# The first head's levels and states ahead of the split of the combined x, in one line that orders a half's mix

## The chip, the cores and the metric

The kernel runs on one core of a Trainium2 chip. Its time is the device time of one execution in microseconds (us), as a median of several runs; lower is better. Beside the runs there is one profiled execution, from which the views of the trace come. The engines are PE (matrix products, with PEld loading weights beside it), DVE (vector work), ACT (activations, copies, casts), POOL and SP (which issues most DMAs). Each has its own queue of instructions and takes them strictly in order; an instruction that waits holds up all behind it on its engine.

## The reference

One decoder layer over x of (1, 2048, 1024) in float32. Two groups of heads read the same normed x, their outputs are joined, projected and added; a gated MLP with a causal convolution follows.

```python
u = rmsnorm(h, norm_mix_w)
proj = u @ w_in                        # hq, hf, hi, hg: 4 heads of 128 each; att: 8 query heads, 2 key/value heads of 64
f = lb + (1 - lb) * sigmoid(hf)        # forget gates; k = 1 - f
o_hg = hgrn2_chunkwise(q, k, v=hi, log(f))   # S_t = diag(f_t) S_{t-1} + k_t v_t^T, o_t = S_t^T q_t
o_hg = rmsnorm(o_hg, hg_norm_w) * silu(hg)
o_att = sliding_window_attention_with_sinks(aq, ak, av, sinks)   # window of 128, blocks of 128 queries
h = h + concat(o_hg, o_att) @ w_out
v = rmsnorm(h, norm_ffn_w)
h = h + (silu(conv(v @ w_gate)) * (v @ w_up)) @ w_down
out = rmsnorm(h, final_norm_w)
```

## The kernel before

The layer runs over two halves of 1024 tokens. Each half has a mix stage (both groups of heads) and an ffn stage (out-projection `pop`, gate and up, down). The features lie on the partitions, the tokens along the free axis, so x is eight tiles of 128 by 1024. Every float32 product is made of three matmuls over rounded parts: high times high, low times high, high times low (lines 933, 934 and 935, with `whi`, `wlo` for a weight and `XH`, `XL` for x). Line 983 rounds on ACT, line 984 takes the rest on DVE.

The mix stage is written as Python generators that a loop advances by the words of the string `ORDER`:

- `H0` to `H3` are the four recurrent heads (`hgrn`), of seven steps each. Step 1 makes q and the forget gates, step 2 the products QK and the first scores in a strip, steps 3, 4 and 5 each two levels of a doubling scheme (1 to 4, 8 and 16, 32 and 64). At a level ACT copies half of QK into a tile `G` (line 718, a ring of three), DVE multiplies (line 722), and PE forms the scores of two levels in one bank, `plev` (line 704). The levels go by the length of a piece, so that of 64 is the last. Step 6 makes the values v, transposes the keys (`pkn`, line 769, copied by ACT to `Kn`) and forms the states (`pu`, line 778; DVE adds them up in `SS`, line 782). Step 7 makes the output (`po`, lines 793 and 794; normed to `on`, line 802; transposed as `pot`, line 807).
- `A0` to `A3` are pairs of attention heads (`attend`), of five steps: the projections (step 1, which also makes the gates of the recurrent heads, tile `hg`), the scores `psc` and softmax `sc` of each 512 queries (steps 2 and 3; lines 545 to 585), then for each 512 the transposes `ppt` (line 594), two masks on DVE (`pp` and `po`, line 597) and the output `poT` (line 607; steps 4 and 5).
- `W0` and `V0` prepare and form the values of the recurrent heads.
- `T0` (`Twofold.begin`) and `U0` (`Twofold.end`) serve a saving of matmuls for pairs of weights: `two_units` uses seven products of quarter size where eight would be needed (accumulators X, Y, Z and V). It needs sums and differences of pieces of x, the combined x. `T0` makes most of them in their own tiles, and `t1` aside; `U0` splits `t1` into its parts and writes them over x's own second half in `X[0]` and `X[1]`, which only the products ahead of it may still read as x.
- `S` loads and splits the finished head outputs for the out-projection.

The kernel doesn't fix each engine's order by hand. A scheduler with a timing model of its own takes the instructions in the order in which the Python code wrote them as priorities and sets each engine's queue, once, at build time. A change of `ORDER` changes these priorities, the choice of buffers and with both the queues. Banks are scarce: four PSUM banks for projections, two for the recurrent heads (`plev`, `pkn`, `pu`, `po`, `pot` share them), two for attention (`psc`, `ppt`, `poT` share them).

Of the kernel before, what the change touches and what calls it, by code (L numbers as in the profile page):

```python
# [20 lines left out]
S = 2048  # L21
# [23 lines left out]
TAIL_WARM = 7  # L45
LV = 4
ORDER = """
H0 W0 T0 H0 V0 U0 H0 A0 H0 H0 H1 A0 A0 H0 H0 H1 A0 H1 A1 H1 A0 H1 H2 A1 A1 H1 H1 H2 A1 H2 A2 H2 A1 H2 H3 A2 A2 H2 H2 H3 A2 H3 A3 H3 A2 H3 A3 A3 S H3 A3 H3 A3
"""
SPLIT = (0, 4, 1, 5, 2, 6)  # L50
DEEP = 2
# [1526 lines left out]
```

## Time and profile before

| | |
|---|---|
| Time before, median of 3 runs | 2173.33 us (2171.72 to 2174.48) |
| Profiled execution, its own time | 2180.96 us |
| Its span, first to last instruction | 2179.2 us |
| Mean granted clock of PE | 0.985 |
| PE busy | 2120.0 us, 97% of the span |
| DVE busy | 1664.7 us, 76% |
| ACT busy | 1136.6 us, 52% |
| First mix, about | 55 to 390 us of the span |
| Second mix, about | 1130 to 1475 us of the span |

A row of the timeline has the start in us from the span's first instruction, the duration in us, the engine, the line of the kernel, the operation, what it writes and reads, its size and how many like it stand together. In brackets stands the engine's idle time just ahead of it and what ended it: `[2.45 <-ACT hg L948]` says that PE stood still for 2.45 us until ACT's line 948 had written `hg`. In a row of the windows each engine has its busy time and in brackets its count of instructions; the granted clock is 1.00 at full speed.

### The profile page before, as it was taken

The numbers are of one execution on the slowest core, as the hardware profiler recorded it, in microseconds if no ns is written. First come the engines' busy times: TensorE is split into PE (matmuls) and PEld (weight loads), VectorE is DVE, ScalarE is ACT, GpSimd is POOL, SyncE is SP. The second block draws the span as 40 slices with busy tenths as digits, with TensorE's granted clock in tenths as the row PEclk, the third lists the DMA queues.
The fourth block names the chain that finished last, engine by engine and source line by source line (L and its number), as shares of the span: only waits on it lengthen the run. The fifth ranks groups of instructions, "written<-read, shape, count | busy, mean of one in ns | idle before, by whom it ended". The sixth has DMA issues, their size and how long they took to land.

```text
span 2179.2 us, 30013 instructions
## 1 busy us (share of the span) xinstructions
PE 2120.0 (97%) x11396; PEld 1747.9 (80%) x11396; DVE 1664.7 (76%) x2453; ACT 1136.6 (52%) x2007; POOL 23.8 (1%) x52
## 2 busy tenths in 40 slices
PE   9999988999999999999999999889999999999998
PEld 7887777788888888888877878668888888888887
DVE  7668887699787878785872568776998888787866
ACT  6576666464444445345744666654644344453454
POOL 1000000000000000000000000000000000000000
PEclk9999998999999999999999999889999999999999
DMA  5544332513233234964652333224132323259743
GB/s 195 185 169 173 116 108 87 188 64 126 92 105 103 100 118 159 389 214 164 224 203 100 114 110 137 86 89 144 59 135 82 126 92 113 95 189 379 247 145 131
DMA packets 116925, 319.19 MB, mean 146 GB/s; under 512 B 19626, under 2 KB 22058, under 8 KB 116780
## 3 DMA queue, kind: packets, MB, share of 16 engines
q1 hardware_dynamic: 111524, 315.42, 41.5%
q10 hardware_dynamic: 5256, 1.85, 0.3%
q8 instruction: 89, 1.46, 0.3%
q14 instruction: 56, 0.46, 0.1%
HBM read 224.21 MB, written 92.02 MB: 145 GB/s over the span
## 4 chain that ended last, share of the span: by engine, by line
PE 72%; DMA 5%; DVE 4%; ACT 4%; issue 1%; SPq 0%; ACTq 0%; DVEq 0%
PE X L1158 7%; PE X L1159 7%; PE X L1160 7%; PE pop L249 5%; PE Y L1160 4%; PE Y L1159 4%; PE Y L1158 4%; PE pdx L1376 3%; PE pdx L1377 3%; PE pdx L1378 3%; PE pdy L1377 3%; PE pdy L1376 3%; PE pdy L1378 3%; PE Z L1160 2%; PE Z L1159 2%; PE Z L1158 2%
## 5 line engine op out<-in xcount | busy, mean ns | idle before, releaser
L983 ACT CAST whi<-raw 128x1024 fp32r<-128x1024 f32 (+2 forms) x123 | 114.5, 941 | 130.4 <-PE X L1159 74.4
L984 DVE TENSOR_TENSOR wlo<-raw,whi 128x1024 fp32r<-128x1024 f32 (+2 forms) x123 | 132.3, 1080 | 9.1 <-ACT whi L983 9.1
L1158 PE MATMUL X<-T,whi 128*128 128x512 f32 x352 | 137.4, 390 | 0.0
L1159 PE MATMUL X<-T,whi 128*128 128x512 f32 x352 | 137.1, 389 | 0.0
L1160 PE MATMUL X<-T,wlo 128*128 128x512 f32 x352 | 137.0, 389 | 0.0
L1257 DVE SCALAR_TENSOR_TENSOR y<-ga,cw,y 128x1024 f32<-128x1024 f32 x88 | 112.3, 1278 | 25.7 <-ACT y L1255 25.7
L1165 ACT COPY u<-X 128x512 f32<-128x512 f32 x88 | 51.6, 587 | 120.5 <-PE X L1160 120.4
L249 PE MATMUL pop<-XH,whi 128*128 128x512 f32 x256 | 86.9, 406 | 4.5 <-ACT XH L618 1.7
L249 PE MATMUL pop<-XL,whi 128*128 128x512 f32 x256 | 87.5, 405 | 1.5 <-DVE XL L261 0.9
L984 DVE TENSOR_TENSOR xld<-raw,xhd 128x1024 fp32r<-128x1024 f32 x72 | 80.2, 1129 | 9.7 <-ACT xhd L983 9.5
L249 PE MATMUL pop<-XH,wlo 128*128 128x512 f32 x256 | 85.9, 400 | 0.0
L983 ACT CAST xhd<-raw 128x1024 fp32r<-128x1024 f32 x72 | 69.2, 979 | 29.4 <-DMA raw<-act0B 7.7
L722 DVE TENSOR_TENSOR QK<-QK,f 128x1024 f32<-128x1024 f32 x56 | 68.3, 1220 | 18.6 <-ACT G L718 18.5
L1158 PEld LDWEIGHTS X<-T,whi 128*128 128x128 f32 x352 | 66.0, 188 | 15.2 <-ACT u L1165 1.6
L1160 PEld LDWEIGHTS X<-T,wlo 128*128 128x128 f32 x352 | 66.1, 188 | 13.8
L1159 PEld LDWEIGHTS X<-T,whi 128*128 128x128 f32 x352 | 66.1, 188 | 13.7
L718 ACT COPY G<-QK 128x1024 f32<-128x1024 f32 x48 | 51.6, 1075 | 46.6 <-DVE QK L722 38.6
L1377 PE MATMUL pdx<-xld,hid 128*128 128x512 f32 x192 | 74.7, 389 | 0.0
L1376 PE MATMUL pdx<-xhd,hid 128*128 128x512 f32 x192 | 74.2, 390 | 0.0
L1378 PE MATMUL pdx<-xhd,lod 128*128 128x512 f32 x192 | 72.4, 389 | 0.0
L1160 PE MATMUL Y<-B,S 128*128 128x512 f32 x176 | 68.6, 390 | 0.0
L1160 PE MATMUL Z<-B,wlo 128*128 128x512 f32 x176 | 68.5, 389 | 0.0
(468 smaller groups left out, 6442.1 us busy)
## 6 DMA issues: line engine op xcount, KB each, us to landing
wr<-in_w_down SPq DMA_DIRECT2D x90, 512.0 KB
raw<-in_w_gate SPq DMA_DIRECT2D x44, 512.0 KB
raw<-in_w_up SPq DMA_DIRECT2D x44, 512.0 KB
raw<-act0T SPq DMA_DIRECT2D x20, 512.0 KB
raw<-act1T SPq DMA_DIRECT2D x20, 512.0 KB
act0B<-y SPq DMA_DIRECT2D x33, 256.0 KB
act1B<-y SPq DMA_DIRECT2D x33, 256.0 KB
raw<-in_w_out SPq DMA_DIRECT2D x16, 512.0 KB
```

The lines of the kernel that those rows point to most:

```text
L249: marks["unit"] = nc.tensor.matmul(o[b], w, x[:, bs], start=f, stop=l)
L718: nc.scalar.copy(G.rearrange("p t (b c m) -> p t b c m", c=2, m=m), far)
L722: done = nc.vector.tensor_tensor(own, own, Fv.rearrange("p b w -> p w b").unsqueeze(3).to_broadcast([P, 2, nb, m]), op=ALU.mult)
L983: return (nc.scalar.copy(h, src), (eng or nc.vector).tensor_tensor(l, src, h.bitcast(F32), op=ALU.subtract))
L984: (eng or nc.vector).tensor_tensor(l, src, h.bitcast(F32), op=ALU.subtract))
L1158: nc.tensor.matmul(o, wh[:, ws], xh, start=i == 0 and not more, stop=False, skip_group_check=more)
L1159: nc.tensor.matmul(o, wh[:, ws], xl, start=False, stop=False, skip_group_check=more)
L1160: r = nc.tensor.matmul(o, wl[:, ws], xh, start=False, stop=i == 3, skip_group_check=more)
L1257: nc.vector.scalar_tensor_tensor(y, g[:, w:w + HALF], C.cw[:, ft, w:w + 1], y, op0=ALU.mult, op1=ALU.add)
L1376: nc.tensor.matmul(o, wh[:, i, c], ah[:, i, cols], start=f, stop=False, skip_group_check=more)
L1377: nc.tensor.matmul(o, wh[:, i, c], al[:, i, cols], start=False, stop=False, skip_group_check=more)
L1378: nc.tensor.matmul(o, wl[:, i, c], ah[:, i, cols], start=False, stop=l, skip_group_check=more)
```

## The change

Only the string `ORDER` differs:

```diff
 ORDER = """
-H0 W0 T0 H0 V0 U0 H0 A0 H0 H0 H1 A0 A0 H0 H0 H1 A0 H1 A1 H1 A0 H1 H2 A1 A1 H1 H1 H2 A1 H2 A2 H2 A1 H2 H3 A2 A2 H2 H2 H3 A2 H3 A3 H3 A2 H3 A3 A3 S H3 A3 H3 A3
+H0 W0 T0 H0 V0 H0 H0 H0 U0 H0 A0 H1 A0 A0 H0 H1 H1 A1 H1 A0 H1 H2 A0 A1 A1 H1 H1 H2 A1 H2 A2 H2 A1 H2 H3 A2 A2 H2 H2 H3 A2 H3 A3 H3 A2 H3 A3 A3 S H3 A3 H3 A3
 """
```

The first head's steps 3, 4 and 5 (levels) and 6 (states) now stand ahead of the first attention pair, and three of them ahead of `U0`; before, `U0` stood ahead of step 3, and steps 4 to 6 stood among the first pair's. Behind that, the first pair's outputs (its steps 4 and 5) stand later: step 4 behind the second head's step 4 (before ahead of its step 3), step 5 behind the third head's first. From `A1 A1 H1 H1` on the words are the same. The same string serves both halves. The instructions that are issued are the same but for six more ACT table loads. On each engine the queues are the same up to the split in the first mix, and again in both ffn stages.

On DVE, at the split in the first mix, `t` is `t1` of the combined x. These rows stand in both kernels, at the same place of the queue; the last is the product of level 16:

```order
L984 TENSOR_TENSOR XL<-t_602,XH 128x512
L984 TENSOR_TENSOR wlo<-raw,whi 128x512 x2
L984 TENSOR_TENSOR XL<-t_617,XH 128x512
L984 TENSOR_TENSOR wlo<-raw,whi 128x512 x2
L722 TENSOR_TENSOR QK<-QK,f 128x2x32x16
```

The split did not move. The product of level 64 on DVE (`QK<-QK,f 128x2x8x64`) stood here before:

```order
L984 TENSOR_TENSOR wlo<-raw,whi 128x768
L547 TENSOR_TENSOR ql<-att_948,qh 64x512
L899 TENSOR_TENSOR raw<-raw 128x256
L903 TENSOR_TENSOR raw<-raw 128x256
L547 TENSOR_TENSOR ql<-att_948,qh 64x512
L693 COPY_PREDICATED strip<-lmask_327,odd 126x32x2
L900 TENSOR_TENSOR raw<-raw 128x256
L693 COPY_PREDICATED strip<-lmask_333,odd 124x16x4
L952 TENSOR_TENSOR att_948<-att_948,Y 128x512
L904 TENSOR_TENSOR raw<-raw 128x256
L528 SCALAR_TENSOR_TENSOR att_948<-att_948,invb 128x512
L722 TENSOR_TENSOR QK<-QK,f 128x2x8x64
```

and stands here now:

```order
L746 TENSOR_TENSOR F<-f 128x8
L528 SCALAR_TENSOR_TENSOR att_1078<-att_1078,invb 128x512
L563 MEMSET sc 128x128 x2
L722 TENSOR_TENSOR QK<-QK,f 128x2x8x64
L547 TENSOR_TENSOR ql<-att_1078,qh 64x512 x2
L693 COPY_PREDICATED strip<-lmask_327,odd 126x32x2
L984 TENSOR_TENSOR wlo<-raw,whi 128x768
L693 COPY_PREDICATED strip<-lmask_333,odd 124x16x4
L899 TENSOR_TENSOR raw<-raw 128x256
```

It came forward over the split of a weight, the low parts of the queries (`ql`) and the four sums of a combined weight (lines 899 to 904).

On PE, in the second mix, the scores of a pair in the half's early part (`psc`), and what stands ahead of them, before:

```order
L933 MATMUL X<-XH,whi 128x512
L934 MATMUL X<-XL,whi 128x512
L704 MATMUL plev<-G 64x64 x8
L704 MATMUL plev<-G 32x32 x16
L558 MATMUL psc<-KS,qh 128x256
L558 MATMUL psc<-KS,ql 128x256
```

The first scores of the same pair now:

```order
L933 MATMUL Z<-XH,whi 128x512
L558 MATMUL psc<-KS,qh 128x256
L934 MATMUL Z<-XL,whi 128x512
L935 MATMUL Z<-XH,wlo 128x512
L933 MATMUL Y<-XH,whi 128x512
L934 MATMUL Y<-XL,whi 128x512
L558 MATMUL psc<-KS,qh 128x256
L935 MATMUL Y<-XH,wlo 128x512
```

Before, a batch of eight scores stands ahead of these X products, and the next batch of eight follows right behind `plev`. Now `plev` has gone ahead, and the first scores of the batch stand singly among Z and Y products.

On PE, in the second mix's last part, the transposes `ppt` of a pair's first 512 queries and the output `poT` from them, before (`pop` is the out-projection, its numbers are accumulators):

```order
L594 MATMUL ppt<-ident,sc 128x128 x5
L249 MATMUL pop_12741<-XL,whi 128x512
L249 MATMUL pop_12742<-XL,whi 128x512
L249 MATMUL pop_12741<-XH,wlo 128x512
L249 MATMUL pop_12742<-XH,wlo 128x512
L249 MATMUL pop_12783<-XL,whi 128x512
L249 MATMUL pop_12784<-XL,whi 128x512
L249 MATMUL pop_12783<-XH,wlo 128x512
L249 MATMUL pop_12784<-XH,wlo 128x512
L704 MATMUL plev<-G 64x64 x8
L704 MATMUL plev<-G 32x32 x16
L607 MATMUL poT<-pp,V 64x128 x2
```

and now:

```order
L793 MATMUL po<-v_12534,ST 128x128
L794 MATMUL po<-SS,QK 128x128
L249 MATMUL pop_12784<-XH,wlo 128x512
L594 MATMUL ppt<-ident,sc 128x128 x8
L607 MATMUL poT<-pp,V 64x128 x2
```

Eight out-projection products and a `plev` stood between the transposes and the output. Now the output follows the transposes directly, and the out-projection products and `plev` stand ahead of both.

## The prediction

> **What bounds the kernel now.** I read the busy table first, then the clock row and the chain of waits, to see which engine sets the end.
>
> ```profile
> PE 2120.0 (97%) x11396; PEld 1747.9 (80%) x11396; DVE 1664.7 (76%) x2453; ACT 1136.6 (52%) x2007; POOL 23.8 (1%) x52
> PEclk9999998999999999999999999889999999999999
> PE 72%; DMA 5%; DVE 4%; ACT 4%; issue 1%; SPq 0%; ACTq 0%; DVEq 0%
> ```
>
> PE is busy for 2120.0 us of a span of 2179.2 us. The change adds no matmul, so it can gain only from the 59.2 us in which PE stands still, and from stretches in which the clock is low. The next view, the table of windows, shows where these lie. Its columns are the stretch and its length, busy time of PE, PEld, DVE, ACT and POOL, the granted clock, the DMA share and GB/s.
>
> ```profile
> 180.00:240.00 60.00, 55.79 (x513) 45.81 (x511) 47.86 (x101) 43.45 (x113) 1.55 (x3) 1.00 0.39 139
> 240.00:300.00 60.00, 56.71 (x469) 46.56 (x470) 47.49 (x99) 41.64 (x84) 0.00 (x0) 0.97 0.44 160
> 300.00:345.00 45.00, 34.10 (x265) 28.65 (x264) 36.17 (x72) 26.87 (x67) 1.55 (x3) 0.77 0.30 96
> 1140.00:1180.00 40.00, 39.97 (x248) 32.24 (x246) 10.78 (x15) 13.52 (x37) 0.00 (x0) 1.00 0.20 63
> 1290.00:1345.00 55.00, 51.07 (x359) 43.94 (x356) 37.15 (x80) 35.79 (x98) 2.09 (x3) 0.97 0.28 97
> 1345.00:1400.00 55.00, 51.08 (x461) 42.20 (x462) 40.61 (x84) 34.01 (x95) 1.95 (x3) 0.94 0.23 81
> 1400.00:1475.00 75.00, 60.03 (x512) 47.69 (x507) 55.62 (x112) 44.68 (x110) 0.00 (x0) 0.84 0.38 122
> ```
>
> PE's idle time in the three stretches of the first mix is 4.2, 3.3 and 10.9 us (length less busy time), and in the last three of the second 3.9, 3.9 and 15.0 us: 41.2 us of the 59.2. That is the stock from which this change draws. In both tails the clock is low as well, 0.77 and 0.84. At 1140 to 1180 us, where the second mix splits the combined x, PE stands still for 0.03 us.
>
> **The split itself: nothing.** The words of the change speak of the first head's levels standing ahead of the split. DVE's timeline at both splits, with the idle time before an instruction and its releaser in brackets:
>
> ```profile
> 96.42 0.69 DVE L984 TENSOR_TENSOR XL<-t,XH 128x512 fp32r<-128x512 f32 x1 [7.63 <-ACT XH L983]
> 102.28 1.22 DVE L722 TENSOR_TENSOR QK<-QK,f 128x1024 f32<-128x1024 f32 x1 [2.16 <-ACT G L718]
> 1175.56 1.29 DVE L984 TENSOR_TENSOR XL<-t,XH 128x512 fp32r<-128x512 f32 x2 [24.45 <-ACT XH L983]
> 1181.42 1.22 DVE L722 TENSOR_TENSOR QK<-QK,f 128x1024 f32<-128x1024 f32 x1 [4.57 <-ACT G L718]
> ```
>
> DVE had been idle for 7.63 and 24.45 us when the split came, and it idles again before the next level: the level waits for its G, not for the split. In the order of the changed kernel the split's rows stand where they stood, ahead of the product of level 16; only the product of level 64 comes forward, over some ten rows of work on weights and attention. With PE full at that place, I cost all of this at 0. If that cover were gone, the price would be the split's two pieces, 2 x 0.69 = 1.4 us in each mix. What the change does lies behind it: the first head's later products come forward in the queues, and attention goes back. The sum is over PE's waits there, one by one.
>
> **First mix.** PE's timeline at its waits, with one row of low clock (243.37) and one transpose (306.52):
>
> ```profile
> 221.38 0.38 PE L558 MATMUL psc<-KS,qh 128*128 128x256 f32 x1 [1.29 <-DVE sc L567]
> 236.87 0.44 PE L607 MATMUL poT<-pp,V 128*64 128x128 f32 x4 [0.83 <-DVE pp L597]
> 241.07 0.50 PE L933 MATMUL Y<-XH,whi 128*128 128x512 f32 x1 [2.45 <-ACT hg L948]
> 241.41 0.39 PE L934 MATMUL Y<-XL,whi 128*128 128x512 f32 x1
> 241.64 0.40 PE L935 MATMUL Y<-XH,wlo 128*128 128x512 f32 x1
> 243.37 0.63 PE L935 MATMUL Y<-XH,wlo 128*128 128x512 f32 x1
> 299.42 1.16 PE L778 MATMUL pu<-v,Kn 128*128 128x128 f32 x8 [2.21 <-ACT Kn L770]
> 306.52 0.60 PE L594 MATMUL ppt<-ident,sc 128*128 128x128 f32 x4
> 311.26 0.69 PE L607 MATMUL poT<-pp,V 128*64 128x128 f32 x4 [4.14 <-DVE pp L597]
> 327.26 0.44 PE L607 MATMUL poT<-pp,V 128*64 128x128 f32 x4 [4.00 <-DVE pp L597]
> ```
>
> (a) 221 to 241 us, together 4.6 us. In the new order the second attention output of pair 0 has whole groups of Y, X and V products between its transposes and itself, so its 0.83 us goes. The Y product that waited 2.45 us for ACT's copy has some seven products of 512 columns more ahead of it, and these follow each other in 0.23 us (241.41 to 241.64): 1.6 us. I take -0.8 - 1.6 = -2.4 us; ends -4.6 and 0.
>
> (b) 299 to 327 us, together 10.35 us. Here both orders have nearly met again. The state product pu keeps some 0.6 us more ahead of it (2.21 to 1.6). The 4.14 us wait is handed on rather than removed: with poT out of the way the next Y product stands ahead of its ACT copy, which queues behind work that came forward, some 3.0 us. The last poT keeps its round trip from ppt over two DVE masks, and one more ACT operation in it (4.00 to 4.6). -1.1 us; ends -4 and +2.
>
> **Second mix.** The same view:
>
> ```profile
> 1293.88 0.57 PE L558 MATMUL psc<-KS,qh 128*128 128x256 f32 x1 [2.80 <-DVE sc L567]
> 1307.63 1.16 PE L778 MATMUL pu<-v,Kn 128*128 128x128 f32 x8 [1.13 <-ACT Kn L770]
> 1373.53 2.08 PE L778 MATMUL pu<-v,Kn 128*128 128x128 f32 x8 [3.18 <-ACT Kn L770]
> 1402.94 0.38 PE L558 MATMUL psc<-KS,qh 128*128 128x256 f32 x1 [1.50 <-ACT qh L546]
> 1405.47 0.38 PE L558 MATMUL psc<-KS,ql 128*128 128x256 f32 x1 [1.53 <-ACT ql L548]
> 1407.51 0.58 PE L558 MATMUL psc<-KS,qh 128*128 128x256 f32 x1 [1.06 <-DVE sc L567]
> 1435.22 0.87 PE L594 MATMUL ppt<-ident,sc 128*128 128x128 f32 x3 [3.24 <-DVE sc L585]
> 1448.81 0.50 PE L249 MATMUL pop<-XH,whi 128*128 128x512 f32 x1 [1.06 <-ACT XH L618]
> 1462.22 1.97 PE L807 MATMUL pot<-ident,on 128*128 128x128 f32 x8 [3.48 <-DVE on L802]
> ```
>
> (c) 1293 and 1307 us: 2.80 + 1.13 = 3.93 us. Today two batches of eight score products have only the plev row between them, so the second waits for DVE to empty a bank. In the new order single scores stand among Z and Y products, and pu has twelve X and Z products and a whole poT between pkn and itself. I keep 1.4 us for banks that come free late all the same: -2.5 us; ends -3.9 and 0.
>
> (d) 1373 us: 3.18 us. Products of heads 1 and 2 come forward while attention goes back, and about half of the wait finds work: -1.5 us; ends -3.2 and +2.
>
> (e) 1402 to 1408 us: 1.50 + 1.53 + 1.06 = 4.1 us, the scores of the last pair waiting for their operands. In the new order out-projection products (pop) that need nothing from them stand around them. 1 us stays: -3 us; ends -4.1 and 0.
>
> (f) The tail, 3.24 + 1.06 + 3.48 = 7.8 us. The wait of ppt for the scores stays (3.24): the scores come later, and so do the products ahead of ppt. Behind it a new wait opens: eight transposes and directly behind them poT, with nothing between, which in the first mix cost 4.14 us. The second poT has two pops and eight pot between; that pot took 1.97 us at the low clock (1462.22), half of it at the full one, so with the pops some 2.1 us, and 2.0 us of the 4.1 shows. The 1.06 stays, the 3.48 goes, since the head's output stands much earlier. 3.24 + 4.14 + 2.0 + 1.06 = 10.4, so +2.6 us; ends -5 and +8.
>
> **(g) Table loads.** The order has the same instructions but for six more ACT table loads, three in each mix. ACT's timeline around one, and two of the groups of loads in the first mix (count, busy time, mean ns):
>
> ```profile
> 151.31 0.37 ACT L566 COPY sc<-psc 128x256 f32<-128x256 f32 x1 [0.33 <-PE psc L558]
> 151.70 1.28 ACT L582 ACT_TABLE_LOAD   x1
> 152.99 0.21 ACT L582 ACTIVATE es<-es 128x8 f32<-128x8 f32 x1
> L533 ACT ACT_TABLE_LOAD x4 | 5.1, 1283 | 0.1
> L582 ACT ACT_TABLE_LOAD x4 | 5.1, 1283 | 0.1
> ```
>
> Six loads are 6 x 1.283 = 7.7 us of ACT. ACT is about half idle, but of the 33.9 us of waits shown above ACT ends 13.1 (2.45, 2.21, 1.13, 3.18, 1.50, 1.53 and 1.06), a share of 0.39. By that share 0.39 x 7.7 = 3.0 us reach PE; ends 0 and 7.7.
>
> [...]
>
> **(h) Clock.** Behind the gap of 2.45 us a product takes 0.63 us (243.37) where one took 0.40 (241.64); eight such in a row cost 8 x 0.23 = 1.8 us. Gaps go in (a), (c) and (d), and one opens in (f): on balance I take half of such a stretch, -1 us; ends -3 and +2.
>
> [...]
>
> Sum: -2.4 - 1.1 - 2.5 - 1.5 - 3.0 + 2.6 + 3.0 - 1.0 = -5.9 us. All of it is worked out on the profiled execution, of 2180.96 us, which becomes 2175.1. That execution lies 7.6 us over the median of the runs, 2173.33 us, so I take the difference over to the median: 2167.4 us. About 0.2% (4.35 us) is what a measurement of this kernel can tell from no change: faster is below 2169.0, slower above 2177.7.
>
> **Rivals.** (1) No change, about 2173. The split doesn't move in the queues, so the change does not do what its words say, and the waits only change hands, as in (b). For it: both orders meet again at the end of the first mix, and the tail of a mix is a chain from scores to output with little else left. Against it: the rows of (c) and (e) have a visible cause, batches of scores back to back, and that cause is gone. Price 0, with (a) to (e) eaten by (f) and (g).
>
> (2) Slower, about 2181: the second mix's tail becomes the bound. Attention stands 7 to 15 us of PE work further back there, and the chain of pair 3 (scores, softmax, ppt, masks, poT, pop) ends last. Two groups of DVE and ACT in this tail price its first part:
>
> ```profile
> L570 DVE TENSOR_REDUCE m<-sc 128x8 f32<-128x1024 f32 x2 | 2.4, 1220 | 0.0
> L580 ACT ACTIVATE sc<-sc,m 128x128 f32<-128x128 f32 x16 | 6.2, 388 | 0.0
> ```
>
> One reduction (1.22 us), eight exponentials with their sums (8 x 0.39 and as many reads, about 4.6 us), a division like the reduction (1.2 us) and copies (0.8 us) are near 8 us. A round trip of ppt and masks (4.7 us, from 306.52 to 311.26) and the outputs (2 us) follow: some 14.8 us, against about 10.3 us of matmuls left behind the last scores (fourteen po, sixteen ppt, thirty-two poT and eight pot at 0.11 us, from four poT in 0.44 us at 327.26, are 7.7; eleven pops at 0.23 are 2.6). It decides from the point where ppt waits more than today's 3.24 us by the 4.5 us that these differ. With that 4.5, one table load (1.3), the new 2.6 of (f) and (e) worth nothing, and half of (a) to (d) (-3.7) beside the 3.0 of (g), the sum is +7.7: 2181.
>
> (3) Much faster, about 2158: the waits of (a), (c), (d) and (e) go altogether (4.6 + 3.9 + 3.2 + 4.1 = 15.8 us), table loads stay hidden, (f) costs 2.6 and the clock gives 2: -15. For it: each of these is a wait with free work elsewhere in the mix. Against: removed waits here tend to be handed to the next in line, as DVE is busy for 0.74 of the last stretch.
>
> **Numbers.** My forecast gets 0.40, rival 1 0.26, rival 2 0.24, rival 3 0.10. Faster than 2169.0: forecast and rival 3, 0.50; same 0.26; slower 0.24. The range reaches 2155 (near rival 3, by the lower ends of two or three terms) to 2181 (rival 2); the forecast's own range is 2161 to 2170.
>
> **What would show it.** Right: at about 1290 us no psc wait of over 1 us, psc at the last pair without the three waits, a new poT wait of about 4 us directly behind eight ppt in the second tail, DVE idle before the split as now, the first mix's last poT waiting about 4 us. Wrong: the chain of waits in the second tail passing through L585 with over 8 us at one ppt, or PE's idle time in both mixes unchanged at 41 us in other places.

## The result, and the profile after

| | before | changed |
|---|---|---|
| Median | 2174.48 us (5 runs, 2171.72 to 2177.66) | 2164.3 us (5 runs, 2162.6 to 2166.7) |
| Ratio | | 0.9951, 95% interval 0.9937 to 0.9966 |
| Span of the profiled execution | 2179.2 us | 2161.1 us |

The change makes the kernel 10.2 us faster. The forecast was 5.9 us faster, 2167.4 us, worked from a median of 2173.33 us of three runs. From the median of five it would be 2168.6 us, so the change brought 4.3 us more than was forecast. The profiled execution of before (2180.96 us) lies above its median and that of the changed kernel (2162.86 us) below, so the spans differ by more, 18.1 us, than the medians do.

The first rows of the changed kernel's page, as shown of before:

```profile
PE 2104.0 (97%) x11396; PEld 1739.0 (80%) x11396; DVE 1664.1 (77%) x2453; ACT 1144.2 (53%) x2013; POOL 24.9 (1%) x52
PE 74%; DVE 5%; ACT 3%; DMA 3%; issue 1%; SPq 0%; ACTq 0%; DVEq 0%
```

PE stands still for 57.1 us of the span (2161.1 less 2104.0), against 59.2 before: nearly as long. What fell is PE's busy time itself, by 16 us, for the same matmuls. The table of windows over each whole mix, first of before and then of the changed kernel (stretch, length, busy time of PE, PEld, DVE, ACT and POOL, granted clock), shows where:

```profile
55.40:453.20 397.80, 374.66 (x2664) 308.20 (x2663) 300.16 (x576) 249.43 (x576) 5.12 (x9) 0.97 0.41 145
1130.80:1537.60 406.80, 381.61 (x2680) 312.56 (x2679) 259.75 (x495) 224.18 (x533) 6.06 (x9) 0.95 0.34 118
```

```profile
55.00:450.10 395.10, 372.37 (x2664) 306.42 (x2663) 299.66 (x576) 253.25 (x579) 6.04 (x9) 0.97 0.41 146
1127.70:1519.50 391.80, 368.57 (x2679) 305.46 (x2678) 259.40 (x496) 228.61 (x536) 5.67 (x9) 0.97 0.36 123
```

A mix is taken here from its first value product to the first product of the gates in the ffn stage behind it. The first mix lost 2.7 us, the second 15.0. In the second, PE's idle time (length less busy) went from 25.2 to 23.2 us only, while the granted clock rose from 0.95 to 0.97. The ffn stages between and behind the mixes are as long as before, within 0.1 us.

The same windows that the prediction used, of the changed kernel:

```profile
180.00:240.00 60.00, 58.21 (x512) 47.95 (x512) 45.00 (x92) 41.93 (x98) 2.01 (x3) 1.00 0.42 153
240.00:300.00 60.00, 54.64 (x486) 44.90 (x486) 48.55 (x106) 45.85 (x98) 0.00 (x0) 0.97 0.44 160
300.00:345.00 45.00, 35.44 (x345) 29.03 (x344) 41.15 (x80) 31.70 (x79) 2.01 (x3) 0.85 0.34 109
1290.00:1345.00 55.00, 53.73 (x505) 44.90 (x503) 45.95 (x96) 38.79 (x99) 2.10 (x3) 1.00 0.34 118
1345.00:1400.00 55.00, 43.60 (x334) 37.10 (x329) 41.00 (x86) 39.83 (x102) 1.56 (x3) 0.91 0.27 92
1400.00:1475.00 75.00, 68.21 (x508) 56.81 (x509) 53.35 (x106) 46.51 (x114) 0.00 (x0) 0.95 0.37 121
```

Idle time of PE in these six, before and after: 4.2 to 1.8, 3.3 to 5.4, 10.9 to 9.6, 3.9 to 1.3, 3.9 to 11.4, and 15.0 to 6.8 us. A good half of the second mix's idle time now stands in one place, 1380 to 1401 us (12.1 of 23.2 us). PE's timeline there and behind it, in the changed kernel:

```profile
1382.73 0.44 PE L607 MATMUL poT<-pp,V 128*64 128x128 f32 x4 [2.48 <-DVE pp L597]
1387.82 1.25 PE L807 MATMUL pot<-ident,on 128*128 128x128 f32 x8 [1.83 <-DVE on L802]
1395.53 1.08 PE L704 MATMUL plev<-G 128*32 128x32 f32 x64 [5.36 <-ACT G L718]
1400.95 2.08 PE L249 MATMUL pop<-XH,whi 128*128 128x512 f32 x4 [2.44 <-ACT XH L260]
1413.79 0.39 PE L558 MATMUL psc<-KS,ql 128*128 128x256 f32 x1 [0.18 <-ACT ql L548]
1419.46 0.39 PE L558 MATMUL psc<-KS,qh 128*128 128x256 f32 x1 [0.32 <-DVE sc L567]
1439.77 0.44 PE L607 MATMUL poT<-pp,V 128*64 128x128 f32 x4 [3.18 <-DVE y L188]
```

The scores of the last pair wait 0.5 us in place of 4.1, and the poT directly behind its transposes waits 3.18 us. The wait of 5.36 us is new. ACT's timeline shows what stood ahead of its copy:

```profile
1386.02 0.58 ACT L612 COPY att<-poT 128x512 f32<-128x512 f32 x1 [1.47 <-PE poT L607]
1386.62 1.28 ACT L582 ACT_TABLE_LOAD   x1
1387.92 0.21 ACT L582 ACTIVATE es<-es 128x8 f32<-128x8 f32 x1
1388.13 1.28 ACT L533 ACT_TABLE_LOAD   x1
1389.43 0.63 ACT L533 ACTIVATE hg<-hg 128x512 f32<-128x512 f32 x1
1390.06 1.28 ACT L580 ACT_TABLE_LOAD   x1
1391.36 0.40 ACT L580 ACTIVATE sc<-sc,m 128x128 f32<-128x128 f32 x1
...
1394.45 1.03 ACT L718 COPY G<-QK 128x1024 f32<-128x1024 f32 x1
```

One small exponential, one silu of a gate, then the softmax's exponentials: three table loads within 4.7 us, and the copy that `plev` needs comes last. In before's queue one silu load and one exponential load stand at this place; two of the three are among the six that the new order added.

### The profile page after: what moved, and what is told of

It reads as the page before. It is cut to its first block, busy times and chain, and to the rows that moved or that the text cites. A ratio compares the mean times of both kernels' runs of the same rounds, so it can differ in the third digit from the quotient of the medians.

```text
span 2161.1 us, 30017 instructions
## 1 busy us (share of the span) xinstructions
PE 2104.0 (97%) x11396; PEld 1739.0 (80%) x11396; DVE 1664.1 (77%) x2453; ACT 1144.2 (53%) x2013; POOL 24.9 (1%) x52
## 4 chain that ended last, share of the span: by engine, by line
PE 74%; DVE 5%; ACT 3%; DMA 3%; issue 1%; SPq 0%; ACTq 0%; DVEq 0%
PE X L1158 7%; PE X L1159 7%; PE X L1160 7%; PE pop L249 6%; PE Y L1160 4%; PE Y L1158 4%; PE Y L1159 4%; PE pdx L1376 3%; PE pdx L1378 3%; PE pdx L1377 3%; PE pdy L1376 2%; PE pdy L1377 2%; PE pdy L1378 2%; PE Z L1159 2%; PE Z L1160 2%; PE Z L1158 2%
## 5 line engine op out<-in xcount | busy, mean ns | idle before, releaser
L1158 PEld LDWEIGHTS X<-T,whi 128*128 128x128 f32 x352 | 66.1, 188 | 15.1 <-ACT u L1165 1.6
L1159 PEld LDWEIGHTS X<-T,whi 128*128 128x128 f32 x352 | 66.1, 188 | 13.6
L718 ACT COPY G<-QK 128x1024 f32<-128x1024 f32 x48 | 51.6, 1076 | 41.9 <-DVE QK L722 30.5
```

Source lines behind the costliest of these rows:

```text
L718: nc.scalar.copy(G.rearrange("p t (b c m) -> p t b c m", c=2, m=m), far)
L1158: nc.tensor.matmul(o, wh[:, ws], xh, start=i == 0 and not more, stop=False, skip_group_check=more)
L1159: nc.tensor.matmul(o, wh[:, ws], xl, start=False, stop=False, skip_group_check=more)
```

## Experiments

All ratios are to runs of before that were taken beside them; their median was 2174.48 us for the changed kernel and 2176.94 to 2177.97 us for the other rows. The stage lengths come from one profiled execution of each, and two executions with the same queues differ by up to 4.5 us in a mix (406.8 and 402.3). "Half clock" adds up the stretches in which the trace records a granted clock of 0.5; idle is length less PE's busy time in the window of the mix.

| words of first, second half | ratio (95% interval) | first mix: us, idle, half clock | second mix: us, idle, half clock |
|---|---|---|---|
| old, old (before) | 1 | 397.8, 23.1, 23.9 | 406.8, 25.2, 37.5 |
| split moved alone | 1.0008 (0.9995 to 1.0021) | 396.9, 20.7, 27.3 | 402.3, 22.8, 30.7 |
| new, old | 0.9991 (0.9979 to 1.0003) | 395.7, 22.9, 20.5 | 404.3, 23.5, 34.1 |
| old, new | 0.9955 (0.9938 to 0.9971) | 395.2, 23.9, 17.1 | 391.3, 24.1, 17.1 |
| new, new (changed) | 0.9951 (0.9937 to 0.9966) | 395.1, 22.7, 20.5 | 391.8, 23.2, 20.5 |
| all but the split | 0.9955 (0.9939 to 0.9970) | 398.1, 25.9, 17.1 | 394.9, 24.5, 27.3 |
| first head's words alone | 0.9968 (0.9956 to 0.9979) | 404.7, 25.0, 37.5 | 392.5, 22.9, 17.1 |
| later words alone | 0.9962 (0.9949 to 0.9976) | 405.4, 25.5, 34.1 | 390.8, 19.1, 17.1 |
| new, later words alone | 0.9937 (0.9924 to 0.9950) | 399.2, 25.1, 23.9 | 388.5, 18.2, 13.7 |

### Does the place of the split matter?

The split is moved alone, over the first head's step 3:

```diff
 H0 W0 T0 H0 V0
-U0 H0
+H0 U0
 A0
...
```

> The order of before, with the split of the combined x moved behind the first head's step 3 and nothing else. Queue theory (the split waits for nothing that anyone needs, the gain comes from the steps behind it): the queues of all engines come out as before's, so ratio 1.000 within 0.2%, some 2174 us. Split theory (levels ahead of the split is what pays, as the words of the change say): a part of the gain, 2 to 5 us faster, 2169 to 2172 us.

And everything but the split is changed:

```diff
 H0 W0 T0 H0 V0
-U0 H0 A0 H0 H0 H1 A0 A0 H0 H0 H1 A0 H1 A1 H1 A0 H1 H2
+U0 H0 H0 H0 H0 A0 H1 A0 A0 H0 H1 H1 A1 H1 A0 H1 H2 A0
...
```

> The change with the split put back to where it stood, ahead of the first head's step 3; all other words as in the change. Queue theory: the queues come out as the changed kernel's, so 2164 us, 0.9951 within 0.2%. Split theory: part of the gain is lost, 2167 to 2172 us.

Measured 1.0008 and 0.9955. The queues that were built settle it beside the times: with the split moved alone, every engine's queue is before's, row for row, and with everything but the split, it is the changed kernel's. The split's place in the words does nothing, since in the queues it stands ahead of the same products in both. What it would cost to move the split itself in a queue, no run shows. DVE's timeline at the second split of the changed kernel:

```profile
1172.85 1.29 DVE L984 TENSOR_TENSOR XL<-t,XH 128x512 fp32r<-128x512 f32 x2 [24.45 <-ACT XH L983]
1178.71 1.23 DVE L722 TENSOR_TENSOR QK<-QK,f 128x1024 f32<-128x1024 f32 x1 [4.57 <-ACT G L718]
```

DVE idles for the same 24.45 and 4.57 us around it as before.

### Which half?

`ORDER` becomes a pair of strings, one for each half. The changed words stand in the first half alone, then in the second alone:

```diff
...
-            for n, step in enumerate(ORDER.split()):
+            for n, step in enumerate(ORDER[hf].split()):
```

> The changed order in the first half, before's order in the second. In the two profiles the first mix became 2.7 us shorter (397.8 to 395.1) and the second 15.0 us (406.8 to 391.8), of which the medians (10.2 us in all) bear out some two thirds. Second-mix theory: 2 to 3 us faster than before, about 2172 us. Theory of equal shares (the profiles of one execution exaggerate the second mix): 5 us faster, 2169 us. If the order of the first mix spoiled the start of the second through buffers, slower than 2174.

> Before's order in the first half, the changed order in the second. Second-mix theory: 7 to 9 us faster than before, 2165 to 2167 us, with the second mix near 392 us and the first near 398 us. Equal shares: 5 us, 2169 us. The gains of the two halves should add up to the whole of 10 us.

Measured 0.9991 (no change that can be told) and 0.9955. The second half carries the gain. Beside one another, the three kernels with the old words in the second half have second mixes of 406.8, 402.3 and 404.3 us, mean 404.5, with 23.8 us of idle time and 34.1 us of half clock; the three with the new words have 391.8, 394.9 and 391.3, mean 392.7, with 23.9 us idle and 21.6 us of half clock. So 11.8 us went without any change in idle time. (PE's queues in these second mixes are alike but not equal: with the first half alone 23 of some 2680 matmuls stand elsewhere than in before, with the second half alone 88 elsewhere than in the changed kernel.)

Part of a stretch at half clock is idle time, which is counted already, so only PE's busy time within it tells what the clock costs. Here are one such stretch and the sum of all in the second mix, of before and then of the changed kernel (stretch, length and busy times as in the windows above):

```profile
1433.87:1440.70 6.83, 5.11 (x77) 4.06 (x78) 6.83 (x13) 1.61 (x3) 0.00 (x0) 0.50 0.01 3
sum 37.55, PE 32.04 PEld 26.29 DVE 30.37 ACT 17.14 POOL 0.00; mean PE 5.34 PEld 4.38 DVE 5.06 ACT 2.86 POOL 0.00
```

```profile
1393.46:1407.11 13.65, 9.14 (x170) 7.77 (x172) 11.21 (x23) 7.32 (x16) 0.00 (x0) 0.50 0.23 78
sum 20.47, PE 15.32 PEld 12.77 DVE 17.99 ACT 9.74 POOL 0.00; mean PE 5.11 PEld 4.26 DVE 6.00 ACT 3.25 POOL 0.00
```

With the old words PE was busy at half clock for 32.0, 27.9 and 30.5 us, with the new for 11.6, 15.3 and 19.1 us: 14.8 us less on average. At half clock products of 512 columns follow each other in 0.43 us in place of 0.23 (at 310 to 314 us of the changed kernel), so about half of that time is lost, and the clock gave 7.4 us. PE's busy time less this lost half, its time as if at full clock, is 365.5 to 365.6 us in the three old mixes and 360.9 to 361.3 us in the three new ones. That is the other 4.5 us: the same matmuls followed each other in shorter steps. Most of it lies with small products of the recurrent heads; from start to start, as if at full clock, the 128 products into `po` took 15.1 us before and 13.5 us in the changed kernel, and those into `plev` 11.4 and 10.2 us. Why their new places shorten these steps stays open.

### Which words?

The first head's words alone:

```diff
 H0 W0 T0 H0 V0
-U0 H0 A0 H0 H0 H1 A0 A0 H0 H0 H1 A0
+H0 H0 H0 U0 H0 A0 H1 A0 A0 H0 H1 A0
 H1 A1 H1 A0 H1 H2
...
```

> Of the change only its first words: the first head's levels and states ahead of the first attention pair, in both halves; the order of the first pair's outputs and the second head's steps behind it as before. If the gain comes from the first head's early levels and states (pu and G copies out of the way of the scores), most of the 10 us: 0.9955 to 0.997. If it comes from the later words (the first pair's outputs behind the second head's levels), none: 1.000 within 0.2%, some 2176 us.

The later words alone:

```diff
 H0 W0 T0 H0 V0 U0 H0 A0 H0 H0 H1 A0 A0 H0 H0 H1
-A0 H1 A1 H1 A0 H1 H2
+H1 A1 H1 A0 H1 H2 A0
...
```

> The other part of the change alone: the first head as before, and only the later words changed (the first pair's two outputs behind the second head's levels). If the later words carry the gain: 0.9955 to 0.997. If the first head's words do: 1.000 within 0.2%. If the two need each other, neither this nor the run of the first words alone comes near 0.9955.

Measured 0.9968 and 0.9962: neither group carries the gain by itself, since each alone brings some 7 us. The windows over both mixes, of the first head's words and then of the later words, show why they don't add up:

```profile
54.90:459.60 404.70, 379.74 (x2663) 312.41 (x2662) 301.04 (x576) 249.68 (x576) 6.06 (x9) 0.95 0.41 142
1137.20:1529.70 392.50, 369.65 (x2680) 306.28 (x2678) 258.43 (x496) 225.96 (x535) 5.59 (x9) 0.98 0.36 122
```

```profile
55.30:460.70 405.40, 379.90 (x2663) 311.35 (x2662) 300.71 (x576) 250.71 (x576) 6.04 (x9) 0.96 0.41 142
1138.40:1529.20 390.80, 371.67 (x2680) 306.70 (x2679) 259.34 (x497) 229.83 (x537) 6.08 (x9) 0.98 0.36 123
```

In the second mix either group of words is enough: 392.5 and 390.8 us. They get there in different ways. With the first head's words PE's time as if at full clock falls to 361.6 us, with 22.9 us idle; with the later words it stays at 364.9 us and the idle time falls to 19.1 us. Busy time at half clock is short in both, 16.1 and 13.6 us. In the first mix either alone costs some 8 us (404.7 and 405.4 against 395 to 399), mostly at a low clock (37.5 and 34.1 us at half clock against 17.1 to 27.3), and only both together cost nothing. What the words do is thus not a property of a word, but of the whole queue that comes out.

That a mix goes by its own queue can be tried: the changed words in the first half, the later words alone in the second.

> The changed order in the first half, the later words alone in the second; the queues of the first mix are the changed kernel's and those of the second are the ones of the run of the later words alone. In that run the first mix took 405.4 us and the second 390.8; the changed kernel's first mix takes 395 to 398. If a mix's length goes by its own queue: first mix near 396, second near 391, 13 to 15 us faster than before, ratio near 0.9935. If the length of the second mix hangs on where the clock's stretches fall after the first: anything between 390 and 395, ratio 0.9955.

Measured 0.9937 (0.9924 to 0.9950), as expected from the sum, though the first mix came out some 3 us longer than expected (399.2) and the second 2.5 us shorter (388.5). Its queues in the first mix are the changed kernel's, and in the second those of the later words. Its ratio is below that of both (0.9951 and 0.9962), but the intervals still overlap, so the gain over them is likely and not shown.

### What do the table loads cost?

Sigmoid and silu of the gates become a tanh, and no table load is left in either mix. What these gates compute is then not the reference's; the queues stay the same row for row, less the loads.

```diff
-            nc.scalar.activation(g[:, bs], g[:, bs], AF.Silu)
+            nc.scalar.activation(g[:, bs], g[:, bs], AF.Tanh)
...
-            nc.scalar.activation(f[:, bs], f[:, bs], AF.Sigmoid)
+            nc.scalar.activation(f[:, bs], f[:, bs], AF.Tanh)
```

> Before, with the sigmoid of the forget gates and the silu of the output gates replaced by a tanh, so that these values are not the reference's. The queues of all engines stay word for word the same; only 23 table loads of ACT go (29.5 us of ACT at 1.283 us each), nearly all in the mixes. Term (g) of the prediction (a load reaches PE with a share of 0.39): 11 us faster than before, ratio 0.995. Hidden loads (ACT is half idle): within 0.2%. Loads on the path in full: 20 us or more, since the clock gains with them.

> The changed kernel with the same replacement; 29 table loads go, and its queues stay the same too. Term (g): it gains 0.39 x 6 x 1.283 = 3.0 us more from this than before did, so the change is worth some 13 us where loads cost nothing (against 10 with them). Tail theory from the changed kernel's trace (at 1386 to 1395 us three loads stand in the chain to a plev that waits 5.4 us): the stall there shrinks to under 2 us, the clock stays up behind it, and the gain is 5 to 8 us more than before's. Hidden loads: no difference, the change stays at 10 us.

Before becomes 0.9981 (0.9970 to 0.9991), the changed kernel 0.9898 (0.9881 to 0.9915). In us of 2177, before gains 4 from 23 loads (29.5 us of ACT) and not the 11 us of the share of 0.39: its share is 0.14. The changed kernel goes from 0.9951 to 0.9898 and gains 12 from 29 loads (37.2 us), a share of 0.32. The two intervals of the changed kernel, with loads and without, lie apart. The difference is some 8 us. Put down to the six extra loads alone, it is about as much as they last (7.7 us), against the 3.0 us of the prediction. This is an estimate: by the intervals it is uncertain by some 5 us, and the other 23 loads stand at other places in the changed queue, where they may cost more too. Without loads the order change is worth 18 us (0.9898 over 0.9981). PE's timeline of the changed kernel without loads, at the same place:

```profile
1378.47 0.44 PE L607 MATMUL poT<-pp,V 128*64 128x128 f32 x4 [1.72 <-DVE pp L597]
1383.55 1.97 PE L807 MATMUL pot<-ident,on 128*128 128x128 f32 x8 [3.12 <-DVE on L802]
1387.33 0.76 PE L704 MATMUL plev<-G 128*32 128x32 f32 x64 [0.52 <-ACT G L718]
1392.85 1.73 PE L249 MATMUL pop<-XH,whi 128*128 128x512 f32 x4 [3.74 <-ACT XH L260]
1432.43 0.44 PE L607 MATMUL poT<-pp,V 128*64 128x128 f32 x4 [3.20 <-DVE y L188]
```

The wait of `plev` shrinks from 5.36 to 0.52 us as the tail theory said, though part of it passes to the next `pop` (2.44 to 3.74) and to `pot` (1.83 to 3.12). With the poT ahead of them, the four waits fall from 12.1 to 9.1 us, for three loads of 3.85 us together. The poT behind its transposes waits as long as with loads (3.20 and 3.18 us): that round trip doesn't hang on ACT's tables.

The same end can be had with the reference's result, in part: a sigmoid is half of one plus the tanh of half the argument, and the constants fold into a line that exists.

```diff
-        nc.vector.tensor_scalar(C.omlb, C.lb, -1.0, 1.0, op0=ALU.mult, op1=ALU.add)
+        nc.vector.tensor_scalar(C.omlb, C.lb, -0.5, 0.5, op0=ALU.mult, op1=ALU.add)
+        nc.vector.tensor_tensor(C.lb, C.lb, C.omlb, op=ALU.add)
...
-            nc.scalar.activation(f[:, bs], f[:, bs], AF.Sigmoid)
+            nc.scalar.activation(f[:, bs], f[:, bs], AF.Tanh, scale=0.5)
```

> The changed kernel with the forget gates' sigmoid computed as (1 + tanh(x/2))/2, the constants folded into the line that follows, so the result is the reference's. Queues as in the changed kernel but for one tiny DVE instruction; 12 of the 29 table loads in its mixes go, those of the sigmoid and those that it causes. Equal price per load (12 us for 29 in the run without loads): 5 us, ratio 0.993. If only the loads in the second tail's stall count (exp and silu by turns): 0 to 1 us, ratio 0.995.

Measured 0.9935 (0.9918 to 0.9951), some 3 to 4 us below the changed kernel. Eleven loads went, not twelve (39 to 28 in its trace). The intervals overlap, so this alone decides nothing; the next run gives it a second pair.

> The two runs before together: each half its best words, and the sigmoid as tanh. If gains add, 18 to 20 us faster than before, ratio near 0.991; if they come out of the same stalls, no better than the better of the two.

Measured 0.9915 (0.9902 to 0.9929), median 2158.41 us: 4.2 us below the same words with sigmoid (2162.65 us, 0.9937), and the fastest version that computes the reference. Here twelve loads went (40 to 28). Both pairs point to about 4 us for eleven or twelve loads, though in neither pair the intervals lie apart.

Last, no loads at all between exponentials: the silu as x times one plus a tanh, for one more DVE operation for each piece of a gate, on top of the run before. The missing half goes into the weight of the heads' norm.

```diff
+        nc.vector.tensor_scalar(C.hgw, C.hgw, 0.5, None, op0=ALU.mult)
...
-            nc.scalar.activation(g[:, bs], g[:, bs], AF.Silu)
+            t = p.tile([P, 512], F32, tag="gate", name="gate", bufs=1)
+            nc.scalar.activation(t, g[:, bs], AF.Tanh, scale=0.5)
+            nc.vector.scalar_tensor_tensor(g[:, bs], t, 1.0, g[:, bs], op0=ALU.add, op1=ALU.mult)
```

> Each half its best words, the sigmoid as tanh, and the output gates' silu as x (1 + tanh(x/2))/2 too: no table load is left between exp and the gates, for one more DVE operation of 0.7 us on each 512 columns of a gate (8 in a half, 5.5 us of DVE). The result is the reference's. If loads are what the change lost by (12 us in the run without loads against 5 in before): 20 to 24 us faster than before, ratio 0.989 to 0.991. If DVE, three quarters busy in the tails, becomes the bound instead: 12 to 16 us, 0.993 to 0.9945.

Measured 0.9977 (0.9967 to 0.9988), worse than either theory allowed, and 14 us slower than with the silu and its loads. Of PE's waits in its first mix (waiting tile, releaser, us in total, count, longest) the two longest are DVE's:

```profile
PE ppt L600 <- DVE t L196: 5.6, 1, 5.6
PE pop L253 <- DVE XL L265: 3.5, 1, 3.5
```

Its first mix has 30.3 us of idle time against 22.3 in the run before it, and its second 25.8 against 18.8, with 8 DVE operations more in each. But the new operations also made the scheduler build other queues in both mixes, so whether DVE's time or the other queues cost this stays open.

## Why the prediction was right, and where its terms were not

The direction, the zero for the split and the range held: 2164.3 us lies 3.1 us below the forecast and in the forecast's own range. That the sum came out near is partly luck. The waits, (a) to (f), were to give 7.9 us. Idle time fell by 5.0 us in the six windows of the prediction (41.2 to 36.2) and by 2.4 us over both mixes (48.3 to 46.0), so the prediction's own sign of being wrong, the same idle time in other places, nearly came. What made up for it is the clock, priced at 1.0 us, and shorter steps of PE, which had no term.

- **The split at nothing: right.** Shown by both runs on it and by the unchanged idle times around it. Rival 1 had its first half right (the words don't do what they say) and its conclusion wrong.
- **(a) -2.4 us in the first mix: handed on.** The waits of poT and Y (0.83 and 2.45 us) went, but idle time in 180 to 300 us only fell from 7.5 to 7.2 us. Two waits of the changed kernel took their place:

```profile
262.07 1.06 PE L594 MATMUL ppt<-ident,sc 128*128 128x128 f32 x8 [1.50 <-DVE sc L585]
287.44 1.00 PE L769 MATMUL pkn<-ident,QK 128*128 128x128 f32 x4 [1.62 <-DVE F L746]
```

- **(b) -1.1: near.** The wait of Y for its ACT copy came as said (3.11 us against some 3.0); pu and the last poT waited less than said (0.80 and 3.15 us against 1.6 and 4.6), and small waits opened behind them, so that idle time in 300 to 345 us fell by 1.3 us. On the whole the changed words in the first half alone can't be told from no change.
- **(c) -2.5: right**, 3.9 to 1.3 us in 1290 to 1345 us; the psc wait is gone, and what is left is a wait for a weight. **(e) -3.0: right**, 4.1 to 0.5 us. The wait that is left under (c):

```profile
1304.84 0.50 PE L933 MATMUL V<-T430h,whi 128*128 128x512 f32 x1 [1.27 <-DMA whi<-ag]
```

- **(d) -1.5: wrong in sign.** The step that failed is that heads 1 and 2 coming forward would fill the wait at 1373 us. They did, and in 1345 to 1400 us idle time rose from 3.9 to 11.4 us all the same: with attention further back, PE ran dry some 10 us later, where outputs, a `plev` and a `pop` wait one after another.
- **(f) +2.6: wrong in sign.** The new poT wait came (3.18 us against 4.14 assumed), but the wait for the scores (3.24 us) did not stay, and the second poT waited 0.63 us in place of 2.0, so the tail's listed waits of 7.8 us became 5.1 us (3.18, 0.49, 0.76 and 0.63). The chain of rival 2 did not become the end: no ppt waited over 0.5 us there, probably because the matmuls that came later too cover pair 3's softmax; no run tried that by itself.
- **(g) +3.0: probably mis-sized.** Six loads cost about 8 us by the estimate above. The step that failed is the share: the share of ACT in PE's waits, 0.39, did not hold for the loads of before (0.14), and where three loads stood in a row in the chain of a wait, 3.0 of their 3.85 us came back when they were left out. On ACT itself a load takes 1.30 us from start to start in the rows: a copy ends at 1386.60, the load runs from 1386.62 for 1.28 us, and the next instruction starts at 1387.92.
- **(h) -1.0: mis-sized, and the larger part of the second mix's gain.** With the waits' sum unchanged there (23.8 and 23.9 us of idle time), 14.8 us less of busy time at half clock gave 7.4 us. The prediction had half of one such stretch in balance for (a), (c), (d) and (f). The remaining 4.5 us, PE's shorter steps, stand in no term: the prediction held PE's busy time fixed but for the clock.

So the terms for waits were right or near one by one in (b), (c) and (e), but their sum over the second mix was nearly nothing: most of what was removed in the chain came back later in it. What stayed is that half of the waits now stand together. That this is why fewer stretches at half clock followed is an inference; no run moved the waits alone.

## What to carry to other kernels

Price a wait together with the clock behind it and with the steps of the matmuls around it: at the same idle time the second mix took 392.7 in place of 404.5 us, 7.4 us of it by the clock and 4.5 us by the steps. Look at what a new order does to function switches on the activation engine, since loads in a row ahead of a wait can cost most of their duration (3.0 of 3.85 us at the `plev` here), though the engine is half idle (ACT is busy for 53% of the span). Tune the order of each repetition by itself: the same words cost 8 us in the first half and saved 12 in the second.

## What the hardware did that was not expected

Gaps of the same length did not cost the same clock. In the changed kernel, PE waited 3.11 us ahead of a product at 309.93 us and 3.18 us ahead of the poT at 1439.77 us. A product soon behind the first gap, and the window around the second:

```profile
309.93 0.50 PE L933 MATMUL Y<-XH,whi 128*128 128x512 f32 x1 [3.11 <-ACT hg L948]
312.25 0.63 PE L935 MATMUL Y<-XH,wlo 128*128 128x512 f32 x1
```

```profile
1439.00:1447.00 8.00, 5.29 (x53) 3.99 (x55) 7.80 (x23) 1.97 (x9) 0.00 (x0) 1.00 0.00 0
```

Behind the first gap the products took 0.63 us from 311.4 to 314.8 us; around the second the granted clock is 1.00, though PE was busy for only 5.29 of 8.00 us. The recorded stretches at half clock lie on a grid: within each of the fourteen traces they start at steps of 3.413 us, to 2 ns, and last one step or several (3.41 to 13.65 us in the mixes of before and of the changed kernel). But where a gap falls on this grid does not explain the pair. The first gap leaves PE idle for 1.91 us of the step ahead of the half clock, the second for 1.94 us of a step with full clock behind it. Over the mixes of all fourteen traces, half clock followed each of the 100 steps with more than 1.94 us of idle time, 58 of the 172 with 1.0 to 1.94 us, and 32 of the 2973 with less (in the two of before and the changed kernel: 12 of 12, 13 of 31, and 5 of 418). What decides in between stays open. The gain of this change thus differs from execution to execution: before's profiled second mixes differ by 4.5 us (406.8 and 402.3, the same queues), with 37.5 and 30.7 us of half clock.
